# A hybrid attention layer on one core: the first gate block's weight split tied behind the attention output, the norm weights spread by TensorE, and the opening order of VectorE changed

## The chip, the cores and the metric

The kernel runs on one core of one Trainium2 chip. The metric is the device time of one execution in microseconds (us); it is given as the median of several executions. A profile of one further execution has a span (first to last instruction) that is a little shorter than that execution's own time. Engines are named as in the profile: PE is TensorE, PEld its weight loads, DVE VectorE, ACT ScalarE, POOL GpSimd, SP SyncE, which issues most transfers (DMA).

## What is computed

One transformer layer on 512 tokens of width 1024, all in float32:

```python
h = rmsnorm(x, norm_mix_w)                    # (512, 1024)
z = h @ w_in                                  # 2328 columns: u, v, q, three k/v pairs, gates
a = gmlp_group(u, v, ...)                     # gated mixing inside chunks of 128 tokens, 8 heads
b = nsa_group(q, k_c, v_c, k_s, v_s, k_w, v_w, g_raw, ...)   # compressed, selected, window attention
mix = concat([rmsnorm(a, out_norm_a_w), rmsnorm(b, out_norm_b_w)])
x = x + mix @ w_o
h = rmsnorm(x, norm_ffn_w)
x = x + (silu(h @ w_gate) * (h @ w_up)) @ w_down            # inner width 2816
out = rmsnorm(x, final_norm_w)
```

## The kernel before

**Precision.** A float32 product is made of three matmuls of a reduced format. Each operand is split into a high part (an ACT copy, `copy_a`, line 79) and a low part (a subtraction, `sub`, line 76, mostly on DVE), and `mm3` (lines 114 to 116) adds high by high, high by low and low by high. Every weight block is therefore loaded (`load_raw`, line 87, into one of three raw buffers), split by two instructions (`split`), and only then read by PE. A raw buffer is free for the next transfer once its low part is made.

**Opening.** Tokens come in four tiles `t` of 128. SP issues the transfers of `x` and of the v columns of `w_in` (`wv`) alternately, and after the first `x` tile that of `wbn`, the norm weights `norm_mix_w`, read once for each of the 128 partitions. `START` writes out the order in which ACT and DVE do four steps per tile: `S` (sums of squares on ACT, then the reciprocal root on POOL, line 167), `T` (DVE scales the tile's two halves by root and weight, line 174, and PE transposes them, line 178), `W` (split of the v weights of that number) and `K` (the transposed tile is split into `hTh` and `hTl`). PE then multiplies: `z_v` is the v projection, 96 matmuls of 512 columns. Ahead of it PE runs 24 transposes of the identity (`warm`, line 199) which nothing reads.

**Attention and output projection.** Scores, softmax (`P`), transposes of the probabilities (`ptp`, line 621), their split (`PT`, high on ACT, low on DVE) and the product with the values (`o`, line 641) go unit by unit; units are numbered (PT46 is the last). After the last unit the raw output `oraw3` is put together (DVE line 650) and split into `mixbh` and `mixbl`, and `pto` (line 660) transposes it for the norm. The output projection `po` (`project`) fills PE's gaps: its first half uses `mixa` and needs no attention, its second half uses `mixb` and the weights `wo1..`, whose low parts POOL makes. Then `ffn_norm(t)` forms the second norm of each tile: squares on ACT (`xf`), root on POOL, DVE scaling by `fwb` (line 174), PE transposes `pt_f`, split into `h2h` and `h2l`.

**Feed-forward.** `gate_up(f)` loads and splits the gate and up blocks of 128 columns, f = 0 to 21; `gate_up(0, 0)` and `gate_up(0, 1)` do block 0 in two token halves while the norm of the last tile is still being made. Its two splits are `wg0` and `wu0`. The splits of block 1 are tied behind `last_norm` by an order-only dependency (`after`): the scheduler must place the later instruction behind the earlier one, and no semaphore is added.

Engines run their instructions in the order that the scheduler wrote, so an instruction that waits holds up all that stand behind it on its engine. Names in rows carry no buffer numbers: `wg_s` is wg0's split, `wo_s` a split of an output weight.

Of the kernel before, what the change touches and what calls it, by code (L numbers as in the profile page):

```python
# [8 lines left out]
F32 = mybir.dt.float32  # L9
F32R = mybir.dt.float32r  # L10
AF = mybir.ActivationFunctionType
OP = mybir.AluOpType
# [6 lines left out]
P = 128  # L19
S = 512  # L20
NT = S // P
DM = 1024
KD = DM // P
# [7 lines left out]
C_U, C_V, C_Q, C_KC, C_KS, C_KW, C_G = 0, 512, 1024, 1536, 1792, 2048, 2304  # L31
NG = 24
FFN_GROUPS = (4, 6, 6, 6)
START = (("S", 0), ("T", 0), ("W", 0), ("K", 0), ("S", 1), ("W", 1), ("T", 1), ("S", 2), ("K", 1), ("T", 2),
         ("W", 2), ("S", 3), ("K", 2), ("T", 3), ("W", 3), ("K", 3))
BANKS = (3, 2, 2, 1)
NBIG, NP, NRAW, NSPL, T4, T2 = 11, 3, 3, 4, 3, 4
# [4 lines left out]
def hybrid_gmlp_nsa_kernel(  # L42
# [8 lines left out]
    nc = tc.nc  # L51
    x, out = x[0], out[0]
    w_in, w_o, w_gate, w_up, w_down = w_in[0], w_o[0], w_gate[0], w_up[0], w_down[0]

    cp = ctx.enter_context(tc.tile_pool(name="consts", bufs=1))
# [19 lines left out]
    def sub(o, a, hi, eng=None):  # L75
        return (eng or nc.vector).tensor_tensor(out=o, in0=a, in1=hi.bitcast(F32), op=OP.subtract)  # L76

    def copy_a(o, a):
        return nc.scalar.activation(o, a, AF.Copy)  # L79
# [25 lines left out]
    def load_cols(w, r0, nk, c0, n, name, eng=None, spare=False, behind=None, halves=False):  # L105
        src = w[r0:r0 + nk * P, c0:c0 + n].rearrange("(k p) f -> p k f", p=P)
        return split(load_raw(src, [nk, n], name), [nk, n], name, eng, spare, behind, halves)

    def after(later, earlier):
        tc.add_manual_dep(later.ins, earlier.ins.name,  # L110
                          mybir.DependencyInfo(mybir.DependencyClass.NoSync, mybir.DependencyReason.DATA), reason="order")
# [6 lines left out]
    def bcast_row(vec, n, name, tag=None):  # L118
        t = cp.tile([P, DM if tag else n], F32, name=name, tag=tag or name)[:, :n]
        nc.sync.dma_start(t, bass.AP(tensor=vec.tensor, offset=vec.offset, ap=[[0, P], [1, n]]))  # L120
        return t
# [4 lines left out]
    def xt(t):  # L126
        return x_sb[t // 2][:, t % 2]

    def v_raw(t):
        return load_raw(w_in[t * 256:(t + 1) * 256, C_V:C_V + 512].rearrange("(k p) f -> p k f", p=P),  # L130
                        [2, 512], f"wv{t}")

    wv_raw = []
    for t in range(NT):
        nc.sync.dma_start(xt(t), x[t * P:(t + 1) * P])
        if t == 0:
            wbn = bcast_row(norm_mix_w, DM, "wbn", tag="wb")
        if t < NRAW:
            wv_raw.append(v_raw(t))

    ident = cp.tile([P, P], F32, name="ident")
    make_identity(nc, ident)
    mhalf = cp.tile([P, 1], F32, name="mhalf")
    nc.vector.memset(mhalf, -0.5)

# [24 lines left out]
    def norm_turn(x_t, r, wb, xs, name):  # L170
        pts = []
        for hf in range(2):
            c = slice(hf * 512, hf * 512 + 512)
            nc.vector.scalar_tensor_tensor(out=xs[:, c], in0=x_t[:, c], scalar=r, in1=wb[:, c],
                                           op0=OP.mult, op1=OP.mult)
            pt = bank("T", [P, 4, P], f"pt_{name}_{hf}")
            for k in range(4):
                nc.tensor.transpose(pt[:, k], xs[:, (hf * 4 + k) * P:(hf * 4 + k + 1) * P], ident)
            pts.append(pt)
        return pts  # L180

    def norm_keep(pts, dst_h, dst_l, t):
        for hf, pt in enumerate(pts):
            d = (slice(None), slice(None), slice(t * P, (t + 1) * P))
            copy_a(dst_h[hf][d], pt)
            done = sub(dst_l[hf][d], pt, dst_h[hf][d])
        return done
# [6 lines left out]
    def bank(tag, shape, name):  # L194
        return ps.tile(shape, F32, tag=tag, name=name, bufs=NB[tag])

    warm = bank("O", [P, 4, P], "warm")
    for k in range(24):
        nc.tensor.transpose(warm[:, k % 4], ident, ident)
    hTh = [b8([P, 4, S], F32R, f"hTh{a}") for a in range(2)]  # L200
    hTl = [b8([P, 4, S], F32R, f"hTl{a}") for a in range(2)]
    v_units = []
    with tc.manual_schedule(engines={mybir.EngineType.Activation, mybir.EngineType.DVE}):
        xs, rs, pts = {}, {}, {}

        def start(t):
            xs[t] = t4([P, DM], F32, f"xs{t}")
            rs[t] = rstd_halves(xt(t), xs[t], f"x{t}")

        def turned(t):  # L210
            pts[t] = norm_turn(xt(t), rs[t], wbn, xs[t], f"x{t}")

        def weight(t):
            if t >= NRAW:
                wv_raw.append(v_raw(t))
            v_units.append(split(wv_raw[t], [2, 512], f"wv{t}"))

        for op, t in START:
            if op == "K":
                norm_keep(pts[t], hTh, hTl, t)  # L220
            else:
                {"S": start, "T": turned, "W": weight}[op](t)

# [18 lines left out]
    for t, z in enumerate(zs):  # L242
# [4 lines left out]
        r = rstd_of(ssq, DA, f"v{t}")  # L247
# [51 lines left out]
    NX = NKV * NCMP  # L299
# [16 lines left out]


    sel = cp.tile([2 * NX, NX], F32, name="sel")
    nc.vector.tensor_tensor(out=sel, in0=ident[:2 * NX, 0:NX], in1=ident[:2 * NX, NX:2 * NX], op=OP.add)
    pair = cp.tile([P, 2, 32], F32, name="pair")  # L320
    idv = ident.rearrange("p (a e n) -> p a e n", a=2, e=2)
    nc.vector.tensor_tensor(out=pair, in0=idv[:, :, 0], in1=idv[:, :, 1], op=OP.add)
    pair = pair.rearrange("p a n -> p (a n)")
    KC = cp.tile([P, NKV, 2, P], F32R, name="KC")
    VC = cp.tile([P, NKV, P], F32R, name="VC")
# [94 lines left out]
    ws = t4([P, NH, P], F32, "ws")  # L420
# [12 lines left out]
    for h2 in range(NH // 2):  # L433
        sv = bank("S", [P, 2, NT, HD], f"sv{h2}")
        for hh in range(2):
            h = h2 * 2 + hh
            c = slice(h * HD, (h + 1) * HD)
            mm3(sv[:, hh], wsT[:, 0, h], wsT[:, 1, h], vnh[:, :, c], vnl[:, :, c], True, True)
            nc.vector.scalar_tensor_tensor(out=ua[:, :, c], in0=sv[:, hh], scalar=bsT[:, h:h + 1],
                                           in1=ua[:, :, c], op0=OP.add, op1=OP.mult)  # L440
# [8 lines left out]
    for k in range(4):  # L449
        pt = bank("T", [P, NT, P], f"pta{k}")  # L450
        for t in range(NT):
# [4 lines left out]
                                       in1=mixah[:, k].bitcast(F32), op0=OP.mult, op1=OP.subtract)  # L456
# [153 lines left out]
    PTs, PTC, outs, oraws, rstd_b = {}, {}, {}, {}, [None] * NT  # L610
# [20 lines left out]
    def apply(u):  # L631
        gi, j, br = UNITS[u]
        i, kv, b0 = GROUPS[gi]
        first, last = j == 0 and b0 + br == 0, j is None
        if first:
            outs[i, kv] = bank("O", [P, 4, P], f"o_{i}{kv}")
        o = outs[i, kv]
        of = o.rearrange("p h c -> p (h c)")
        if not last:
            for a in range(2):  # L640
                nc.tensor.matmul(of, lhsT=Vt[:, b0 + br, j, kv], rhs=PTs[u][:, a],  # L641
                                 start=(first and a == 0), stop=False)
            return
        nc.tensor.matmul(of, lhsT=VC[:, kv], rhs=PTC[i], start=False, stop=True)
        if kv == 0:
            oraws[i] = tp.tile([P, 4, P], F32, tag="oraw", name=f"oraw{i}", bufs=2)
        ol = t2([HD, 4, P], F32, f"ol_{i}{kv}")
        copy_a(ol, o[HD:P])
        for par in range(2):
            nc.vector.tensor_tensor(out=oraws[i][par * HD:(par + 1) * HD, 2 * kv:2 * kv + 2],  # L650
                                    in0=o[0:HD, par::2], in1=ol[:, par::2], op=OP.add)
        if kv == 1:
            d = (slice(None), slice(None), slice(i * P, (i + 1) * P))
            copy_a(mixbh[d], oraws[i])
            sub(mixbl[d], oraws[i], mixbh[d])

    def out_norm(i):
        pt = bank("T", [P, 4, P], f"pto{i}")
# [6 lines left out]
    def ffn_norm(t):  # L665
        xs = t4([P, DM], F32, f"xf{t}")
        r = rstd_halves(x2[t], xs, f"f{t}")
        pts = norm_turn(x2[t], r, fwb, xs, f"f{t}")
        return norm_keep(pts, h2h, h2l, t)


# [33 lines left out]
    gu = {}  # L705

    def gate_up(f, part=None):
        if not part:
            ws = [load_cols(w, 0, KD, f * P, P, f"w{'gu'[a]}{f}", spare=f == 0, behind=last_norm if f == 1 else None,
                            halves=f > 0)  # L710
                  for a, w in ((0, w_gate), (1, w_up))]
            gu[f] = ws, [bank("G" if part is None else "S", [P, S], f"gu{f}{a}") for a in range(2)]
        cut = slice(0, S) if part is None else slice(part * 256, part * 256 + 256)
        for (hi, lo), z in zip(*gu[f]):
            for k in range(KD):
                mm3(z[:, cut], hi[:, k], lo[:, k], h2h[k // 4][:, k % 4, cut], h2l[k // 4][:, k % 4, cut],
                    k == 0, k == KD - 1)
# [28 lines left out]
    last_norm = ffn_norm(NT - 1)  # L746
# [143 lines left out]
```

## Time and profile before

| | before |
|---|---|
| median of 3 executions | 624.6 us (622.62, 624.6, 624.99) |
| the profiled execution's own time | 623.25 us |
| its span | 621.5 us |
| mean granted TensorE clock | 0.991 |
| PE busy | 597.8 us, 96% |
| DVE busy | 401.7 us, 65% |
| ACT busy | 297.4 us, 48% |
| POOL busy | 68.5 us, 11% |

The page gives each engine's busy time as a share of the span. 1.75 us lie between the span and the execution's own time. Times in rows are microseconds from the start of the span; mean durations of one instruction are in ns.

### The profile page before, as it was taken

The numbers are of one execution on the slowest core, as the hardware profiler recorded it, in microseconds if no ns is written. First come the engines' busy times: TensorE is split into PE (matmuls) and PEld (weight loads), VectorE is DVE, ScalarE is ACT, GpSimd is POOL, SyncE is SP. The second block draws the span as 40 slices with busy tenths as digits, with TensorE's granted clock in tenths as the row PEclk, the third lists the DMA queues.
The fourth block names the chain that finished last, engine by engine and source line by source line (L and its number), as shares of the span: only waits on it lengthen the run. The fifth ranks groups of instructions, "written<-read, shape, count | busy, mean of one in ns | idle before, by whom it ended". The sixth has DMA issues, their size and how long they took to land.

```text
span 621.5 us, 7683 instructions
## 1 busy us (share of the span) xinstructions
PE 597.8 (96%) x2823; PEld 489.5 (79%) x2823; DVE 401.7 (65%) x728; ACT 297.4 (48%) x547; POOL 68.5 (11%) x113
## 2 busy tenths in 40 slices
PE   6999899998999988999999999999999999999994
PEld 5778778787788766898888888888888888888883
DVE  4752779648988956646694437694446695346696
ACT  5753367648877865344252323353233353233354
POOL 3100100015442571100000000000000000000001
PEclk9999999999999997999999999999999999999998
DMA  8551635533000021069118232028232018320003
GB/s 314 154 142 51 182 107 150 188 125 115 1 2 1 1 63 40 1 174 320 48 44 261 82 94 62 1 89 266 86 100 69 1 70 270 101 67 1 0 2 135
DMA packets 73638, 61.85 MB, mean 100 GB/s; under 512 B 3697, under 2 KB 64129, under 8 KB 73601
## 3 DMA queue, kind: packets, MB, share of 16 engines
q1 hardware_dynamic: 73024, 60.32, 31.1%
q10 hardware_dynamic: 576, 1.05, 0.4%
q8 instruction: 22, 0.36, 0.2%
q14 instruction: 16, 0.12, 0.1%
HBM read 59.27 MB, written 2.10 MB: 99 GB/s over the span
## 4 chain that ended last, share of the span: by engine, by line
PE 84%; DVE 4%; DMA 3%; ACT 3%; POOL 3%; issue 2%; SPq 0%; POOLq 0%; ACTq 0%; DVEq 0%
PE gu L115 13%; PE gu L116 13%; PE gu L114 13%; PE o L641 3%; PE pA L114 3%; PE pA L116 3%; PE pA L115 3%; PE s L547 3%; PE ptp L621 3%; PE po L115 2%; PE po L116 2%; PE po L114 2%; PE pC L116 1%; PE pC L115 1%; PE pC L114 1%
## 5 line engine op out<-in xcount | busy, mean ns | idle before, releaser
L114 PE MATMUL gu<-h2h,wg_h 128*128 128x512 f32 x168 | 65.4, 389 | 0.0
L115 PE MATMUL gu<-h2l,wg_h 128*128 128x512 f32 x168 | 65.4, 389 | 0.0
L115 PE MATMUL gu<-h2l,wu_h 128*128 128x512 f32 x168 | 65.4, 389 | 0.0
L116 PE MATMUL gu<-h2h,wg_l 128*128 128x512 f32 x168 | 65.4, 389 | 0.0
L114 PE MATMUL gu<-h2h,wu_h 128*128 128x512 f32 x168 | 65.4, 389 | 0.0
L116 PE MATMUL gu<-h2h,wu_l 128*128 128x512 f32 x168 | 65.4, 389 | 0.0
L79 ACT ACTIVATE wu_h<-wu_r 128x1024 fp32r<-128x1024 f32 x21 | 22.3, 1061 | 64.7 <-PE gu L115 48.8
L690 DVE TENSOR_TENSOR sg<-gu,sg 128x512 f32<-128x512 f32 x22 | 15.2, 691 | 57.3 <-PE gu L116 56.7
L76 DVE TENSOR_TENSOR wg_l<-wg_r,wg_h 128x1024 fp32r<-128x1024 f32 x21 | 25.7, 1223 | 41.0 <-ACT wg_h L79 40.5
L79 ACT ACTIVATE wg_h<-wg_r 128x1024 fp32r<-128x1024 f32 x21 | 22.3, 1060 | 48.0 <-PE gu L115 40.9
L167 POOL TENSOR_TENSOR rstd_y<-s_y,mhalf 128x1 f32<-128x1 f32 x4 | 3.0, 754 | 346.1 <-DVE s_y L164 341.4
L552 ACT ACTIVATE P<-P,nm 128x128 f32<-128x128 f32 (+3 forms) x64 | 35.5, 559 | 5.2 <-DVE nm L550 4.7
L82 POOL TENSOR_SCALAR P<-P,sm 128x128 f32<-128x128 f32 (+3 forms) x64 | 34.0, 552 | 32.2 <-DVE sm L559 15.0
L116 PEld LDWEIGHTS gu<-h2h,wg_l 128*128 128x128 f32 x168 | 31.5, 188 | 6.6
L116 PEld LDWEIGHTS gu<-h2h,wu_l 128*128 128x128 f32 x168 | 31.5, 188 | 6.6
L115 PEld LDWEIGHTS gu<-h2l,wu_h 128*128 128x128 f32 x168 | 31.6, 188 | 6.5
L114 PEld LDWEIGHTS gu<-h2h,wg_h 128*128 128x128 f32 x168 | 31.6, 188 | 6.5
L114 PEld LDWEIGHTS gu<-h2h,wu_h 128*128 128x128 f32 x168 | 31.5, 188 | 6.5
L115 PEld LDWEIGHTS gu<-h2l,wg_h 128*128 128x128 f32 x168 | 31.5, 188 | 6.5
L641 PE MATMUL o<-PT,Vt 128*128 128x512 f32 x80 | 32.0, 451 | 4.8 <-ACT PT L79 4.6
L550 DVE CUSTOM_DVE_ANT_0 P<-s,maskw 128x128 f32<-128x128 f32 (+3 forms) x64 | 29.5, 481 | 4.1 <-PE s L547 3.6
L76 DVE TENSOR_TENSOR wu_l<-wu_r,wu_h 128x1024 fp32r<-128x1024 f32 x21 | 25.6, 1219 | 4.9 <-ACT wu_h L79 4.9
(505 smaller groups left out, 1504.7 us busy)
## 6 DMA issues: line engine op xcount, KB each, us to landing
wg_r<-in_w_gate_dram SPq DMA_DIRECT2D x22, 512.0 KB, 3.9
wu_r<-in_w_up_dram SPq DMA_DIRECT2D x22, 512.0 KB, 3.8
wd_r<-in_w_down_dram SPq DMA_DIRECT2D x11, 1024.0 KB, 5.0
wo_r<-in_w_o_dram SPq DMA_DIRECT2D x8, 512.0 KB, 4.3
x_sb<-in_x_dram SPq DMA_DIRECT2D x4, 512.0 KB, 9.0
wv_r<-in_w_in_dram SPq DMA_DIRECT2D x4, 512.0 KB, 7.7
wu_r<-in_w_in_dram SPq DMA_DIRECT2D x4, 512.0 KB, 3.7
w1k_r<-in_cmp_k_w_dram SPq DMA_DIRECT2D x4, 512.0 KB, 3.8
```

What stands on the lines that cost most here:

```text
L76: return (eng or nc.vector).tensor_tensor(out=o, in0=a, in1=hi.bitcast(F32), op=OP.subtract)
L79: return nc.scalar.activation(o, a, AF.Copy)
L82: nc.gpsimd.tensor_scalar(out=o, in0=a, scalar1=s, scalar2=1.0, op0=OP.mult, op1=OP.mult)
L114: nc.tensor.matmul(ps, lhsT=sh, rhs=mh, start=first, stop=False, skip_group_check=more)
L115: nc.tensor.matmul(ps, lhsT=sh, rhs=ml, start=False, stop=False, skip_group_check=more)
L116: nc.tensor.matmul(ps, lhsT=sl, rhs=mh, start=False, stop=last, skip_group_check=more)
L547: nc.tensor.matmul(sb, lhsT=q, rhs=KAB[kv][:, a, b0:b0 + nbr, :n], start=(a == 0), stop=(a == 1))
L550: nc.vector.tensor_tensor_reduce(out=pr, in0=sb[:, br], in1=maskw[:, S - n:], scale=-0.125, scalar=BIG, op0=OP.add, op1=OP.min, accum_out= ...
L552: e = nc.scalar.activation(pr, pr, AF.Exp, bias=nm[b], scale=-1.0, accum_out=sm[b])
L621: nc.tensor.transpose(pt[:, hh], src, ident)
L641: nc.tensor.matmul(of, lhsT=Vt[:, b0 + br, j, kv], rhs=PTs[u][:, a], start=(first and a == 0), stop=False)
L690: nc.vector.tensor_tensor(out=own, in0=pg[1], in1=own, op=OP.mult)
```

## The change

Three things are changed.

1. The split of the gate and up weights of block 0 gets an order-only dependency on the low part of the last attention output, `mixbl` of tile 3, which is the last entry of the new list `mixed`. Before it had none.
2. The transfer that wrote `norm_mix_w` into all 128 partitions is gone. One row of 4 KB is loaded into one partition by ACT's queue (`wrow`), and two plain float32 matmuls with a row of ones spread it over the partitions into two PSUM banks (`wbn[0]`, `wbn[1]`), from where DVE reads it. The 24 warm transposes become 6 ahead of the spread and 3 behind it.
3. On DVE, `T` of tile 1 now stands ahead of `W` of tile 1, and the two small sums `sel` and `pair` are tied behind the last `hTl` of the opening.

```diff
-START = (("S", 0), ("T", 0), ("W", 0), ("K", 0), ("S", 1), ("W", 1), ("T", 1), ("S", 2), ("K", 1), ("T", 2),
+START = (("S", 0), ("T", 0), ("W", 0), ("K", 0), ("S", 1), ("T", 1), ("W", 1), ("S", 2), ("K", 1), ("T", 2),
...
+    wrow = cp.tile([P, DM], F32, name="wrow", tag="wb")
+    nc.scalar.dma_start(wrow[0:1], bass.AP(tensor=norm_mix_w.tensor, offset=norm_mix_w.offset, ap=[[0, 1], [1, DM]]))
     for t in range(NT):
         nc.sync.dma_start(xt(t), x[t * P:(t + 1) * P])
-        if t == 0:
-            wbn = bcast_row(norm_mix_w, DM, "wbn", tag="wb")
...
-            nc.vector.scalar_tensor_tensor(out=xs[:, c], in0=x_t[:, c], scalar=r, in1=wb[:, c],
+            nc.vector.scalar_tensor_tensor(out=xs[:, c], in0=x_t[:, c], scalar=r, in1=wb[hf],
...
-    for k in range(24):
-        nc.tensor.transpose(warm[:, k % 4], ident, ident)
+    for k in range(6):
+        warmed = nc.tensor.transpose(warm[:, k % 4], ident, ident)
+    wbn = []
+    for hf in range(2):
+        wbn.append(bank("SM"[hf], [P, 512], f"wbn{hf}"))
+        spread = nc.tensor.matmul(wbn[hf], lhsT=ones, rhs=wrow[0:1, hf * 512:hf * 512 + 512], start=True, stop=True)
+        after(spread, warmed)
+    for k in range(3):
+        after(nc.tensor.transpose(warm[:, k % 4], ident, ident), spread)
...
-            sub(mixbl[d], oraws[i], mixbh[d])
+            mixed.append(sub(mixbl[d], oraws[i], mixbh[d]))
...
-            ws = [load_cols(w, 0, KD, f * P, P, f"w{'gu'[a]}{f}", spare=f == 0, behind=last_norm if f == 1 else None,
-                            halves=f > 0)
+            behind = mixed[-1] if f == 0 else last_norm if f == 1 else None
+            ws = [load_cols(w, 0, KD, f * P, P, f"w{'gu'[a]}{f}", spare=f == 0, behind=behind, halves=f > 0)
```

The first place where instructions move is ACT at the end of the attention, from the copy of probability unit 43 on. Before:

```order
L79 ACTIVATE PT43_2184<-ptp43_2179 128x512
L79 ACTIVATE wg0_s_2564<-wg0_r_2562 128x1024
L79 ACTIVATE PT44_2194<-ptp44_2189 128x512
L79 ACTIVATE PT45_2204<-ptp45_2199 128x512
L79 ACTIVATE wo111_s_2375<-wo111_r_2371 128x1024
L79 ACTIVATE wu0_s_2569<-wu0_r_2567 128x1024
L79 ACTIVATE PT46_2214<-ptp46_2209 128x512
L79 ACTIVATE ol_31_2220<-o_31_2146 64x512
```

And now:

```order
L79 ACTIVATE PT43_2175<-ptp43_2170 128x512
L79 ACTIVATE PT44_2185<-ptp44_2180 128x512
L79 ACTIVATE PT45_2195<-ptp45_2190 128x512
L79 ACTIVATE wo111_s_2366<-wo111_r_2362 128x1024
L79 ACTIVATE PT46_2205<-ptp46_2200 128x512
L79 ACTIVATE ol_31_2211<-o_31_2137 64x512
L79 ACTIVATE mixbh_1166<-oraw3_2095 128x4x128
L157 ACTIVATE junko3_2222,ssq_o3_2223<-pto3_2217 128x512
L164 ACTIVATE xf0_2425,s2_f0_2426<-x2_0_1168 128x512
L79 ACTIVATE wg0_s_2555<-wg0_r_2553 128x1024
L79 ACTIVATE wu0_s_2560<-wu0_r_2558 128x1024
L164 ACTIVATE xf0_2425,s2_f0_2426<-x2_0_1168 128x512
```

The copies of wg0 and wu0 moved from between the last probability copies to between the two halves of the squares of the first feed-forward norm tile.

The second place is DVE a little later, from the last attention output to the scaling of the first feed-forward norm tile (`xf0`). In the kernel before, the two splits stood ahead of this piece, the first behind PT43 and the second behind PT45. Now:

```order
L661 TENSOR_TENSOR oraw3_2095<-o_31_2137,ol_31_2211 64x256 x2
L524 SCALAR_TENSOR_TENSOR x2_0_1168<-po100_2369,rstd_o0_1454,x2_0_1168 128x512
L76 TENSOR_TENSOR mixbl_1167<-oraw3_2095,mixbh_1166 128x4x128
L150 TENSOR_SCALAR ms_o3_2225<-ssq_o3_2223 128x1
L166 TENSOR_SCALAR s2_f0_2426<-s2_f0_2426 128x1
L524 SCALAR_TENSOR_TENSOR x2_0_1168<-po101_2383,rstd_o0_1454,x2_0_1168 128x512
L76 TENSOR_TENSOR wg0_s_2555<-wg0_r_2553,wg0_s_2555 128x1024
L76 TENSOR_TENSOR wu0_s_2560<-wu0_r_2558,wu0_s_2560 128x1024
L524 SCALAR_TENSOR_TENSOR x2_0_1168<-po110_2397,rstd_o1_1657,x2_0_1168 128x512
L168 TENSOR_TENSOR s2_f0_2426<-s2_f0_2426 128x1
L176 SCALAR_TENSOR_TENSOR xf0_2425<-x2_0_1168,rstd_f0_2430,fwb_1174 128x512 x2
```

The low parts of wg0 and wu0 now stand between the first tile's squares and its scaling.

The third place is the start of DVE's program. Before:

```order
L76 TENSOR_TENSOR wv0_s_145<-wv0_r_75,wv0_s_145 128x1024
L319 TENSOR_TENSOR sel_546<-ident_84 124x62
L322 TENSOR_TENSOR pair_548<-ident_84 128x64
L76 TENSOR_TENSOR hTl0_121<-pt_x0_0_134,hTh0_119 128x4x128
L76 TENSOR_TENSOR hTl1_122<-pt_x0_1_140,hTh1_120 128x4x128
L164 TENSOR_SCALAR s2_x1_153<-s2_x1_153 128x1
L166 TENSOR_TENSOR s2_x1_153<-s2_x1_153 128x1
L76 TENSOR_TENSOR wv1_s_160<-wv1_r_78,wv1_s_160 128x1024
L174 SCALAR_TENSOR_TENSOR xs1_152<-x_sb0_70,rstd_x1_157,wbn_73 128x512 x2
```

And now:

```order
L76 TENSOR_TENSOR wv0_s_136<-wv0_r_75,wv0_s_136 128x1024
L76 TENSOR_TENSOR hTl0_112<-pt_x0_0_125,hTh0_110 128x4x128
L76 TENSOR_TENSOR hTl1_113<-pt_x0_1_131,hTh1_111 128x4x128
L166 TENSOR_SCALAR s2_x1_144<-s2_x1_144 128x1
L168 TENSOR_TENSOR s2_x1_144<-s2_x1_144 128x1
L176 SCALAR_TENSOR_TENSOR xs1_143<-x_sb0_70,rstd_x1_148,wbn0_103 128x512
L176 SCALAR_TENSOR_TENSOR xs1_143<-x_sb0_70,rstd_x1_148,wbn1_105 128x512
L76 TENSOR_TENSOR wv1_s_163<-wv1_r_78,wv1_s_163 128x1024
```

The scaling of tile 1 (`xs1`) changed places with the split of wv1, and `sel` and `pair` left this stretch.

## Rows read from the trace of the kernel before

**Rows 1.** The page's first part: busy time, share of the span, instructions.
```profile
PE 597.8 (96%) x2823; PEld 489.5 (79%) x2823; DVE 401.7 (65%) x728; ACT 297.4 (48%) x547; POOL 68.5 (11%) x113
```

**Rows 2.** Waits of PE, whole span: total us, times, longest.
```profile
PE o L641 <- ACT PT L79: 4.6, 1, 4.6
```

**Rows 3.** Busy us of PE, PEld, DVE, ACT, POOL, then PEclk, DMA, GB/s.
```profile
238.00:240.00 2.00, 2.00 (x8) 1.52 (x8) 2.00 (x2) 0.16 (x1) 1.67 (x1) 0.50 0.01 4
242.00:244.00 2.00, 2.00 (x10) 1.65 (x9) 0.22 (x1) 0.46 (x1) 0.00 (x0) 1.00 0.00 0
400.00:500.00 100.00, 100.00 (x441) 82.41 (x440) 62.48 (x88) 36.65 (x50) 0.00 (x0) 1.00 0.30 95
```

**Rows 4.** Timeline, end of attention: start, us, instruction, [idle before <-releaser].
```profile
230.75 0.47 PE L116 MATMUL po<-wo_s,mixal 128*128 128x512 f32 x1
234.24 1.06 ACT L79 ACTIVATE wg_s<-wg_r 128x1024 fp32r<-128x1024 f32 x1 [5.32 <-DMA wg_r<-in_w_gate_dram]
235.20 1.06 ACT L79 ACTIVATE PT<-ptp 128x512 fp32r<-128x512 f32 x2
235.32 1.23 DVE L76 TENSOR_TENSOR wg_s<-wg_r,wg_s 128x1024 fp32r<-128x1024 f32 x1 [5.68 <-ACT wg_s L79]
235.83 0.79 PE L641 MATMUL o<-PT,Vt 128*128 128x512 f32 x1 [4.60 <-ACT PT L79]
236.42 0.63 PE L114 MATMUL po<-wo_s,mixbh 128*128 128x512 f32 x1
236.85 0.63 PE L115 MATMUL po<-wo_s,mixbh 128*128 128x512 f32 x1
237.29 2.38 POOL L76 TENSOR_TENSOR wo_s<-wo_r,wo_s 128x1024 fp32r<-128x1024 f32 x1 [4.72 <-ACT wo_s L79]
238.26 2.49 DVE L76 TENSOR_TENSOR wu_s<-wu_r,wu_s 128x1024 fp32r<-128x1024 f32 x1
...
245.39 0.39 PE L660 MATMUL pto<-ident,oraw 128*128 128x128 f32 x2
245.98 0.69 DVE L76 TENSOR_TENSOR mixbl<-oraw,mixbh 128x512 fp32r<-128x512 f32 x1 [0.45 <-ACT mixbh L79]
248.53 0.55 POOL L167 TENSOR_TENSOR rstd_f<-s_f,mhalf 128x1 f32<-128x1 f32 x1 [1.06 <-DVE s_f L166]
252.01 1.03 PE L178 MATMUL pt_f<-ident,xf 128*128 128x128 f32 x8
```

**Rows 5.** Timeline of the opening.
```profile
4.18 0.63 ACT L162 ACTIVATE xs<-x_sb 128x512 f32<-128x512 f32 x1 [2.12 <-DMA x_sb<-in_x_dram]
5.80 0.56 POOL L167 TENSOR_TENSOR rstd_x<-s_x,mhalf 128x1 f32<-128x1 f32 x1 [4.01 <-DVE s_x L166]
6.69 1.41 DVE L174 SCALAR_TENSOR_TENSOR xs<-x_sb,rstd_x,wbn 128x512 f32<-128x512 f32 x2 [0.98 <-DMA wbn<-in_norm_mix_w_dram]
8.23 1.06 ACT L79 ACTIVATE wv_s<-wv_r 128x1024 fp32r<-128x1024 f32 x1 [2.71 <-DMA wv_r<-in_w_in_dram]
9.20 1.07 ACT L79 ACTIVATE hTh<-pt_x 128x512 fp32r<-128x512 f32 x2
10.47 0.22 DVE L319 TENSOR_TENSOR sel<-ident 124x62 f32<-124x62 f32 x1
13.61 1.40 DVE L174 SCALAR_TENSOR_TENSOR xs<-x_sb,rstd_x,wbn 128x512 f32<-128x512 f32 x2
13.75 0.50 PE L115 MATMUL z_v<-wv_s,hTh 128*128 128x512 f32 x1 [0.76 <-DVE wv_s L76]
```

**Rows 6.** Weight loads of PE in the opening, timeline.
```profile
1.84 4.57 PEld L199 LDWEIGHTS warm<-ident 128*128 128x128 f32 x24 [1.84 <-POOL ident masks.py:199]
7.50 0.42 PEld L178 LDWEIGHTS pt_x<-ident,xs 128*128 128x128 f32 x4 [1.09 <-DVE xs L174]
```

**Rows 7.** Groups by form: name, shape, count, busy us, mean ns, idle before.
```profile
L580 PE MATMUL ptc<-pair,st_sb 128*128 128x64 f32 x32 | 4.2, 265 | 0.0
L513 DVE SCALAR_TENSOR_TENSOR x<-po,rstd_o,x 128x512 f32<-128x512 f32 x8 | 6.0, 748 | 2.8 <-PE po L116 2.8
```

More of the change, by code (lines that the diff above doesn't have):

```diff
@@ L142, in hybrid_gmlp_nsa_kernel @@
     make_identity(nc, ident)
+    ones = cp.tile([1, P], F32, name="ones")
+    nc.vector.memset(ones, 1.0)
     mhalf = cp.tile([P, 1], F32, name="mhalf")
@@ L219, in hybrid_gmlp_nsa_kernel @@
             if op == "K":
-                norm_keep(pts[t], hTh, hTl, t)
+                kept = norm_keep(pts[t], hTh, hTl, t)
             else:
@@ L318, in hybrid_gmlp_nsa_kernel @@
     sel = cp.tile([2 * NX, NX], F32, name="sel")
-    nc.vector.tensor_tensor(out=sel, in0=ident[:2 * NX, 0:NX], in1=ident[:2 * NX, NX:2 * NX], op=OP.add)
+    done = nc.vector.tensor_tensor(out=sel, in0=ident[:2 * NX, 0:NX], in1=ident[:2 * NX, NX:2 * NX], op=OP.add)
+    after(done, kept)
     pair = cp.tile([P, 2, 32], F32, name="pair")
     idv = ident.rearrange("p (a e n) -> p a e n", a=2, e=2)
-    nc.vector.tensor_tensor(out=pair, in0=idv[:, :, 0], in1=idv[:, :, 1], op=OP.add)
+    done = nc.vector.tensor_tensor(out=pair, in0=idv[:, :, 0], in1=idv[:, :, 1], op=OP.add)
+    after(done, kept)
     pair = pair.rearrange("p a n -> p (a n)")
@@ L654, in apply @@
             copy_a(mixbh[d], oraws[i])
-            sub(mixbl[d], oraws[i], mixbh[d])
+            mixed.append(sub(mixbl[d], oraws[i], mixbh[d]))
+    mixed = []
     def out_norm(i):
@@ L667, in ffn_norm @@
         r = rstd_halves(x2[t], xs, f"f{t}")
-        pts = norm_turn(x2[t], r, fwb, xs, f"f{t}")
+        pts = norm_turn(x2[t], r, (fwb[:, 0:512], fwb[:, 512:]), xs, f"f{t}")
         return norm_keep(pts, h2h, h2l, t)
```

## The prediction

> **What bounds the kernel now.** I read the page's busy shares first: PE is busy 96% of the span, every other engine far less [rows 1]. So the time is PE's work plus the moments in which PE has none or runs slowly, and a change pays only there. The waits of PE come next. The longest single one is a product `o` that waits 4.6 us for the ACT copy of a probability tile [rows 2]; the other waits are small, most of them in the opening.
>
> The timeline around that wait shows who is to blame. PE ends its last free output-projection matmul at about 231.0 (it starts at 230.75, and in long dense stretches 441 matmuls take 100 us, 0.227 each) [rows 3, 4]. The transposes for PT44 and PT45 are done by then, but on ACT the copy of wg0 stands ahead of both, and waits 5.32 us for its transfer, which lands at 234.2. PT44 and PT45 run from 235.20, and PE starts again at 235.83. So the 4.6 us come from an instruction that nobody needs for another 30 us.
>
> The stretch behind it costs more. [...] What the stall costs in all follows from a count: from 231.0 until `pto` at 245.39, PE does, by the order of its instructions, 27 matmuls and 6 transposes. At 0.227 and 0.105 (four transposes' loads take 0.42 [rows 6]) that is 6.1 + 0.6 = 6.75 us. It took 14.4. The excess is 7.65: 4.6 of standing still and about 3.05 of slow clock.
>
> Last I read the opening. DVE's first scaling waits for `wbn` until 6.69, although its root is ready at 5.80 + 0.56 = 6.36; the first v weights follow wbn on the queue and land at 8.23, where ACT has waited 2.71 for them [rows 5]. At 13.75 PE waits its last 0.76 for the low part of wv1, and from there it is nearly closed.
>
> **The change, part by part.**
>
> *The tie behind mixbl.* ACT now goes from PT43 straight to PT44 and PT45. Their transposes end at about 230.5 and 231.0, so the high parts (two take 1.06 [rows 4]) come at 231.15 and 231.75 and DVE's low parts, 0.69 each, at 231.85 and 232.5. PE meanwhile has `o` with the high parts and three projection matmuls; by the order it meets each low part within 0.1 us. The copy of wo111 now runs at 231.8 to 232.8 instead of 236.15, so POOL, whose 2.38 us for its low part began at 237.29 [rows 4], ends near 235.2; PE needs it at about 238.0. That wait, which could have taken the old one's place, stays hidden with 2.8 us to spare. I leave 0.2 us for small waits: 7.65 - 0.2 = 7.45 gained. With no idle stretch the clock has no reason to drop.
>
> *The splits in their new place.* Two ACT copies (1.06 each) and two DVE subtractions (1.23 each [rows 4]) now stand inside the first feed-forward norm. Let p be the time at which PE reaches the second pair of `pto`. Until `pt_f` of tile 0 PE then has 2 transposes and 33 matmuls: p + 7.7. On the other side the add for x2's second half waits for nine more matmuls and ends at p + 3.1 (0.75 [rows 7]). ACT copies wg0 from p + 2.1 and wu0 until p + 4.25, and DVE makes their low parts until p + 5.7. Behind them stand the next add (0.75, to 6.45), the sum of squares, POOL's root (0.55 [rows 4]) with its semaphores (to 7.3) and the first scaling (0.75, to 8.05). PE waits 0.35 there, and 0.35 more since the second half comes 0.75 later and four transposes cover 0.42. I take 0.75 lost. In the kernel before, `pt_f` began at 252.01, 6.6 after `pto`, without a wait. The other tiles' scalings come one by one behind 5.5 us of matmuls each and keep their cover. The bounds: 0 if ACT and DVE run a little ahead of this, and 3.25 if both subtractions take 2.49 each, as that of wu0 did while POOL was at work beside it [rows 4]. In the new place POOL has only roots of 0.55, so 1.23 is nearer.
>
> Together 7.45 - 0.75 = **6.7 us** at this place (bounds 4.2 and 7.65).
>
> *The row instead of the broadcast.* The first x tile lands at 4.18, wbn only at about 6.6 [rows 5]. Without it everything queued behind moves up 2.4 us; wv0 lands near 5.9, and ACT need not wait at 8.23. The row itself is not in the trace. Its landing lies between 0 and the 3.4 us that the 512 KB of x needed from its issue at 0.79: 4.2 at the latest. The spread is two plain float32 matmuls. The nearest rows: a plain float32 matmul leaves two records (32 for 16 calls [rows 7]), and a 128-column transpose takes 4.57/24 = 0.19 at the start and 0.105 later [rows 6]. A 512-column record is then four times that, and the spread 4 x 0.42 = 1.7 to 4 x 0.76 = 3.0; below, 0.9 if a record takes the 0.227 of a dense matmul. So the halves are in PSUM between about 4 and 7.2; DVE wants them at 6.4 and 7.1. Reading the weights from PSUM costs nothing that rows show: 748 ns with a PSUM operand [rows 7] against 1.41 us for two from SBUF [rows 5].
>
> [...]
>
> *DVE's order.* With wv0 there early, hTh of tile 0 is bound by its transposes and starts near 7.7 (9.20 before). `sel` and `pair` (0.22 each) leave DVE. Scaling of tile 1 starts at about 11.4 instead of 13.61 (its root is ready at 11.3), while the low part of wv1, behind it, ends at 14.0 instead of 13.7. When PE closes up, at 14.0, it has done 9 of the 96 z_v matmuls and 16 of 32 transposes, against 7 and 8 at 13.75: 2 x 0.227 + 8 x 0.105 - 0.25 = 1.05 gained. Following DVE to its last hTl instead gives 1.3. With the spread at its latest, PE's 3 warm transposes delay `pt_x` of tile 0 by 0.8, and 0.5 to 0.7 is left. I take **1.0 us** (bounds -0.8, with spread and clock both at their slow end, and 2.4, the whole of wbn's transfer). From 14 on PE is closed, and the transfers of the u weights hang on buffers that PE's progress frees, so the gain reaches the attention unchanged.
>
> *Sum.* 1.0 + 6.7 = 7.7. The profiled execution took 623.25; 615.5 for such a one. The median of the runs is 1.35 higher, 624.6, so **616.9 us**. A difference under about 0.5% (3 us) could not be told from no change here.
>
> **Rivals.**
>
> *A: the wait moves to pt_f.* The splits are slow, PE stands 3.25 us at `pt_f`, and 7.7 - 2.5 = 5.2 are left: 619.4; 622.2 if the clock then falls as it did behind the 4.6 (another 2.8). For it: DVE's 2.49 [rows 4]. Against it: POOL is done by then.
>
> *B: the opening loses.* 15 fewer warm transposes and a hole while PE waits for the row leave PE at the lower clock when z_v begins. After the old stall some 13 matmuls ran slowly, 0.2 us each too long: 2.6. Then the opening is 1.6 worse instead of 1.0 better: 619.5. For it: the early transposes take 0.19, later ones 0.105, so PE did start slowly [rows 6]. Against it: z_v's first matmuls wait for ACT and DVE anyway.
>
> *C: slower.* The same mechanism without an end in sight: z_v's beginning stays so thin that the clock stays low through it. At 0.2 us each it needs 38 slow matmuls to eat the 7.7 and 54 to be slower by 0.5%; all 96 give 616.9 + 19.4 = 636. Against it: after the old stall PE resumed at 235.83 and the clock was back at 1.00 in 242 to 244 [rows 3, 4].
>
> [...]
>
> *D: the opening gains all.* The whole 2.4 of wbn comes through: 615.5.
>
> **How the numbers follow.** The forecast has 0.70, A 0.10, B 0.12, C 0.03, D 0.05. The time is the forecast's, 616.9. The range goes down to D less the spread of the runs (0.8 us below their middle mostly): 614.5. Upward it takes in A and B with as much again: 620.3. Outside lie C, A with the low clock and outliers. Faster by over 0.5% means under 621.5: the forecast, D, most of A and B: 0.93. Within it 0.04, slower 0.03.
>
> **What would show it.** Right: no PE wait for PT of more than 0.5 us; a granted clock of 1.00 from 225 to 250; wg0's copy behind the first half of xf0's squares; `pto` to `pt_f` 7.5 to 9 us; z_v's last matmul 0.5 to 1.5 us earlier. Wrong: a wait at `pt_f` over 2 us, z_v matmuls 0.43 apart beyond the first dozen, DVE's first scaling later than 7, or a new PE wait for POOL's wo111.

## The result, and the profile after

The changed kernel takes 616.91 us in the median of 4 runs (616.63 to 618.19), the kernel before 624.29 (622.62 to 624.99) beside it: a ratio of 0.989, 95% interval 0.9865 to 0.9915, so 5.3 to 8.4 us less. The forecast was 616.9. The profiled execution took 617.18 with a span of 615.4, against 623.25 and 621.5: 6.1 less. The total came out as forecast; several of its terms did not, and the experiments are about those.

The first fence is from the page after (busy time), PE's waits, and PE's busy time and granted clock in the stretch of the old stall (columns as in [rows 3]).

```profile
PE 598.2 (97%) x2812; PEld 487.3 (79%) x2812; DVE 400.7 (65%) x729; ACT 297.7 (48%) x547; POOL 68.2 (11%) x113
...
PE ptp L632 <- POOL P L82: 2.8, 5, 0.8
...
PE cps_v L384 <- ACT hid_v L366: 0.4, 1, 0.4
PE z_u L115 <- DVE wu_s L76: 0.4, 1, 0.4
...
PE pt_x L180 <- DVE xs L176: 0.3, 1, 0.3
PE z_v L114 <- ACT wv_s L79: 0.2, 1, 0.2
...
230.00:240.00 10.00, 9.98 (x50) 7.47 (x49) 5.17 (x10) 5.16 (x11) 5.96 (x4) 1.00 0.36 105
240.00:250.00 10.00, 9.96 (x48) 8.00 (x47) 8.12 (x14) 5.04 (x10) 1.31 (x3) 1.00 0.00 0
```

The wait of `o` for PT [rows 2] is gone, no PE wait is over 0.8 us longest but the two fixed ones on POOL's `ident` (1.8) and `ws` (1.6), and the granted clock that was 0.50 [rows 3], with matmuls 0.43 apart instead of 0.227 [rows 3, 4], is 1.00 throughout. The timeline after, in the place of [rows 4]:

```profile
231.16 1.09 ACT L79 ACTIVATE PT<-ptp 128x512 fp32r<-128x512 f32 x2 [1.64 <-PE ptp L632]
231.32 0.47 PE L116 MATMUL po<-wo_s,mixal 128*128 128x512 f32 x1
231.81 0.50 PE L652 MATMUL o<-PT,Vt 128*128 128x512 f32 x1
...
239.28 0.62 ACT L164 ACTIVATE xf<-x 128x512 f32<-128x512 f32 x1
239.90 1.05 ACT L79 ACTIVATE wg_s<-wg_r 128x1024 fp32r<-128x1024 f32 x1
240.85 1.05 ACT L79 ACTIVATE wu_s<-wu_r 128x1024 fp32r<-128x1024 f32 x1
241.27 1.22 DVE L76 TENSOR_TENSOR wg_s<-wg_r,wg_s 128x1024 fp32r<-128x1024 f32 x1
242.40 1.22 DVE L76 TENSOR_TENSOR wu_s<-wu_r,wu_s 128x1024 fp32r<-128x1024 f32 x1
245.01 1.41 DVE L176 SCALAR_TENSOR_TENSOR xf<-x,rstd_f,fwb 128x512 f32<-128x512 f32 x2 [0.67 <-POOL rstd_f L169]
245.91 1.29 PE L180 MATMUL pt_f<-ident,xf 128*128 128x128 f32 x8
246.96 0.47 PE L114 MATMUL po<-wo_s,mixbh 128*128 128x512 f32 x1
...
259.63 0.36 PE L114 MATMUL gu<-h2h,wg_s 128*128 128x256 f32 x1
```

`o` follows the free projection matmul after 0.5 instead of 5.1 us. The copies of wg0 and wu0 stand behind the first half of xf0's squares, as forecast, and both low parts take 1.22, not 2.49. From the start of that free matmul to `pt_f` of tile 0 it is 14.59 us (231.32 to 245.91), before it was 21.26 (230.75 to 252.01): 6.67 less. By the order of instructions the same 56 matmuls and 8 transposes lie in both; at 0.227 and 0.105 they are 13.54 us. The excess over that was 7.72 and is 1.05.

The forecast of 6.7 took in what is lost behind the start of `pt_f` too, so the fair end is the first gate matmul `gu`. It starts at 259.63; before it was

```profile
265.48 0.36 PE L114 MATMUL gu<-h2h,wg_s 128*128 128x256 f32 x1
```

That is 34.73 us from the free matmul before and 28.31 now: **6.42 less, where 6.7 was forecast**. The span shows 6.1: the free matmul itself comes 0.57 later in this execution than in the one before, and 0.25 is won behind `gu`.

The opening after, in the place of [rows 5, 6]:

```profile
3.31 3.77 PE L205 MATMUL wbn<-wrow,ones 1*128 1x512 f32 x4
6.58 1.40 DVE L176 SCALAR_TENSOR_TENSOR xs<-x_sb,rstd_x,wbn 128x512 f32<-128x512 f32 x2 [0.68 <-POOL rstd_x L169]
7.71 1.91 PE L180 MATMUL pt_x<-ident,xs 128*128 128x128 f32 x8
8.81 0.60 ACT L79 ACTIVATE hTh<-pt_x 128x512 fp32r<-128x512 f32 x1 [2.10 <-PE pt_x L180]
9.46 0.79 PE L114 MATMUL z_v<-wv_s,hTh 128*128 128x512 f32 x1
10.05 0.63 PE L115 MATMUL z_v<-wv_s,hTh 128*128 128x512 f32 x1
10.47 0.63 PE L116 MATMUL z_v<-wv_s,hTl 128*128 128x512 f32 x1
12.35 1.40 DVE L176 SCALAR_TENSOR_TENSOR xs<-x_sb,rstd_x,wbn 128x512 f32<-128x512 f32 x2 [0.68 <-POOL rstd_x L169]
12.48 0.49 PE L114 MATMUL z_v<-wv_s,hTh 128*128 128x512 f32 x1 [0.23 <-ACT wv_s L79]
```

The row is there by 3.31, so it does land early; but the spread takes 3.77, and PE works at half its pace long behind it: `pt_x` takes 1.91 instead of 1.32 and the first z_v matmuls stand 0.43 apart. (The windows of this opening say a granted clock of 1.00 throughout, also where the matmuls stand 0.43 apart, so here the pace is read from their distance.) ACT waits 2.10 for `pt_x`, and the scaling of tile 1 comes at 12.35 where 11.4 was forecast. The first matmul of z_u, which follows z_v without a gap, starts at 36.83 instead of 37.24: 0.4 gained, not 1.0.

And this 0.4 does not reach the end of the attention: on ACT the copy of w_k stands ahead of `hid_v`, and its transfer came late.

```profile
111.48 1.06 ACT L79 ACTIVATE w_k_s<-w_k_r 128x1024 fp32r<-128x1024 f32 x1 [0.86 <-DMA w_k_r<-in_w_in_dram]
112.45 0.25 ACT L366 ACTIVATE hid_v<-hps_v 128x124 f32<-128x124 f32 x1
112.75 0.63 PE L384 MATMUL cps_v<-w_v,hid_v 128*31 128x64 f32 x8 [0.44 <-ACT hid_v L366]
```

`cps_v` starts at 112.75, before at 112.76. This goes mostly with the new opening: PE waits 0.2 to 0.6 at this place in all six traces in which the new opening brought the first z_u matmul before 37 (after, and e2, e5, e8, e11 and e12 of the experiments below), and of the eight others only in e4, 0.4. Why the transfer is late there stays open; an early z_u alone does not do it, since e7, which has the earliest, has no such wait.

### The profile page after: what moved, and what is told of

Its sections match the earlier page's. It is cut to its first block, busy times and chain, and to the rows that moved or that the text cites. A ratio compares the mean times of both kernels' runs of the same rounds, so it can differ in the third digit from the quotient of the medians.

```text
span 615.4 us, 7662 instructions
## 1 busy us (share of the span) xinstructions
PE 598.2 (97%) x2812; PEld 487.3 (79%) x2812; DVE 400.7 (65%) x729; ACT 297.7 (48%) x547; POOL 68.2 (11%) x113
## 3 DMA queue, kind: packets, MB, share of 16 engines
q10 hardware_dynamic: 578, 1.05, 0.5%
## 4 chain that ended last, share of the span: by engine, by line
PE 87%; DVE 5%; DMA 2%; POOL 2%; ACT 2%; issue 1%; POOLq 0%; SPq 0%; DVEq 0%; ACTq 0%
PE gu L115 13%; PE gu L116 13%; PE gu L114 13%; PE o L652 3%; PE pA L114 3%; PE ptp L632 3%; PE pA L115 3%; PE pA L116 3%; PE s L558 3%; PE po L115 2%; PE po L116 2%; PE po L114 2%; PE pC L114 2%; PE pC L115 2%; PE pC L116 2%
## 5 line engine op out<-in xcount | busy, mean ns | idle before, releaser
L76 DVE TENSOR_TENSOR PT<-ptp,PT 128x512 fp32r<-128x512 f32 x40 | 26.6, 684 | 5.7 <-ACT PT L79 5.5
```

## The experiments

**One part alone.** First the tie without the opening, and the opening without the tie.

```
# e1: before, and
+            mixed.append(sub(mixbl[d], oraws[i], mixbh[d]))
+            behind = mixed[-1] if f == 0 else last_norm if f == 1 else None
# e2: the changed kernel, with these two undone
```

> The kernel before with the tie behind mixbl alone. Theory (the prediction's terms): -6.7 us, about 617.6 at a median of 624.3, no PE wait for PT, granted clock 1.00 from 225 to 250, pto to pt_f 7.5 to 8. Rival (the opening earned the gain, or the two parts need each other): under 4 us gained here.

> The kernel before with the row, the spread and DVE's order, without the tie. The prediction's term: -1.0 us, 623.3. Theory after the two traces: the gain is 0.5 at the first z_u matmul (36.8 against 37.2) and is taken back at cps_v, where ACT waits for the transfer of w_k_r; 0 in the end, 624.3 +- 0.5. Rival B (the slow PE costs more than the transfer gives): 1.6 worse, 626.

e1: 617.43 against 623.13, ratio 0.9901 (0.9883 to 0.992). e2: 622.94 against the same, ratio 0.9996 (0.9986 to 1.0006). So the tie earns 5 to 7.3 us, and the opening between a loss of 0.4 and a gain of 0.9. In e1's trace, too, it is 14.59 us from the free matmul to `pt_f`. e2's first z_u matmul is at 36.85, and PE waits 0.2 at `cps_v`, so part of that gain is taken back there, as was expected of e2. e1's, which has the opening of before, is at 38.86, 1.6 later than in the execution of before that was profiled (below, matmuls of z_v and windows with columns as in [rows 3]):

```profile
12.15 0.63 PE L114 MATMUL z_v<-wv_s,hTh 128*128 128x512 f32 x1
12.57 0.63 PE L115 MATMUL z_v<-wv_s,hTh 128*128 128x512 f32 x1
...
8.00:10.00 2.00, 0.88 (x7) 0.51 (x5) 0.68 (x2) 1.69 (x3) 1.10 (x4) 1.00 1.04 413
12.00:14.00 2.00, 2.00 (x6) 1.22 (x6) 1.78 (x5) 1.73 (x5) 0.56 (x1) 0.50 1.04 391
14.00:17.00 3.00, 3.00 (x12) 2.42 (x12) 1.32 (x5) 0.60 (x1) 0.55 (x1) 0.50 0.93 279
```

With the same code and the same 24 transposes, PE went through z_v's beginning at half its pace until 17 this time: after a stretch in which it was busy 0.88 of 2 us (0.98 in before) the granted clock fell to 0.50. In e3 it reads 0.50 from 12 to 14, in before 1.00 throughout. So the opening of before is not one number; the three other traces with it (before, e3, e4) have the first z_u matmul at 37.17 to 37.59. With the new opening (after, e2, and e5 below) it is at 36.83, 36.85 and 36.86.

**What the stall cost.** e3 keeps the stall and gives PE something to do in it; e4 leaves the copies untied and takes their transfers away.

```
# e3: before, and in the loop over units, between turn(45) and apply(44);
# not shown: the first o is tied behind the last pad, PT46's transposes behind o
+    pad, prev = bank("S", [P, 4, P], "pad"), turn(45)
+    for k in range(44):
+        pad_mm = nc.tensor.transpose(pad[:, k % 4], ident, ident)
+        after(pad_mm, prev)
+        prev = pad_mm
# e4: before, and in load_cols
+    if spare:
+        return split(fwb.rearrange("p (k f) -> p k f", k=nk), [nk, n], name, eng, spare, behind, halves)
```

> The kernel before with 44 transposes of the identity, into a bank that nobody reads, between the transposes of PT45 and the product o that waits for PT44; PT46's transposes go behind o. The stall stays (ACT still waits for wg0's transfer until 234.2), PE only has something to do in it. Theory (the 3 us behind the stall come from PE having stood still): granted clock stays 1.00 and matmuls 0.227 apart behind 236, about 3 us gained, 621.3. [...]

> The kernel before with wg0 and wu0 split from a tile that landed long ago (the norm's weights), so that their transfers are gone and the first gate block's result is another; no tie, so ACT still has the copies ahead of the PTs. Theory (the wait for the transfer made the stall, not the 1.06 us of each copy): no PE wait for PT over 0.8 us, and no new work inside the first feed-forward norm, 7.5 gained, 616.8. Rival (ACT simply has too much ahead of PT44): a wait of 1 to 2 us stays, with a slow clock behind it, 619 to 621.

e3: 623.04, ratio 1.0 (0.9987 to 1.0012): no gain, yet the clock did not fall. Its timeline of PE, and the window in which the clock was 0.50 before:

```profile
230.95 4.97 PE L744 MATMUL pad<-ident 128*128 128x128 f32 x44
235.76 0.50 PE L644 MATMUL o<-PT,Vt 128*128 128x512 f32 x1
237.14 1.09 PE L644 MATMUL o<-PT,Vt 128*128 128x512 f32 x3 [0.88 <-DVE PT L76]
...
238.00:240.00 2.00, 2.00 (x12) 1.41 (x12) 1.66 (x3) 1.29 (x2) 0.00 (x0) 1.00 0.00 0
```

The granted clock stays 1.00, and behind 238 the matmuls stand 0.227 apart. So the slow clock did come from PE standing still, and 4.8 us of nothing but transposes kept it away; only transposes had run, too, when the loads went from 0.19 to 0.105 us [rows 6]. The count of the same work tells where the gain went: from 230.95 to `pt_f` at 251.29 it is 20.34 us (21.26 before), 6.80 over the 13.54. Of this 4.81 are the transposes put in, 1.15 lie at the new wait (in this kernel's order `o` meets PT44's low part at once, which on DVE stands behind wg0's), and 0.84 remain. So 0.84 of excess is what this stretch costs at full clock, in steps of about 0.1 where PE changes between `po`, `o` and transposes. Before had 7.72 = 4.85 at the stall + 2.87, and by this count the slow clock's share of the 2.87 is about 2.0. Counted by instructions it is 2.6: nine matmuls take 0.20 too long each, a tenth 0.15, and six transposes 0.105 each. Either is less than the 3.05 of the prediction.

e4: 617.83, ratio 0.992 (0.9903 to 0.9937), 4 to 6 us gained. This run changes one thing more: the scheduler puts the copies earlier, behind PT41 and PT42 instead of PT43 and PT45. They still stand ahead of probability copies of the same kind, 1.06 us each, and PE waits for none of those on ACT. But something of the rival is there, on DVE instead of ACT:

```profile
227.87 9.05 POOL L76 TENSOR_TENSOR wo_s<-wo_r,wo_s 128x1024 fp32r<-128x1024 f32 x3
229.51 2.82 DVE L76 TENSOR_TENSOR wu_s<-fwb,wu_s 128x1024 fp32r<-128x1024 f32 x1
232.26 1.27 DVE L76 TENSOR_TENSOR PT<-ptp,PT 128x512 fp32r<-128x512 f32 x2
232.99 0.73 PE L643 MATMUL o<-PT,Vt 128*128 128x512 f32 x2 [1.25 <-DVE PT L76]
```

Beside POOL's subtraction of the same kind wu0's low part takes 2.82, in the changed kernel without POOL 1.22. The low part of a probability tile waits behind it, and PE 1.25. This is rival A's mechanism, found where POOL does work. The transfer made most of the stall; in this order the place next to POOL still costs 1.3 us.

**What the opening is made of.** Beside the changed kernel once more (e5), e6 takes DVE's order back, e9 (later) puts that order alone into the kernel before, e7 leaves the norm's weights out, and e8 uses ACT's idle 2.1 us.

```
# e5: the changed kernel
# e6: START with ("W", 1), ("T", 1) again; e9: before with ("T", 1), ("W", 1) and sel, pair behind kept
# e7: no wrow, no spread; 24 transposes; ones = cp.tile([P, DM], F32, ...) set to 1
+    wbn = [ones[:, 0:512], ones[:, 512:]]
# e8: START = ... ("W", 0), ("S", 1), ("K", 0), ("T", 1), ("W", 1), ...
```

> The changed kernel itself once more, as the measure for the others here: 616.9 +- 1. Its opening: first z_v matmul about 9.5, z_v 0.43 apart until about 12, first z_u matmul near 36.8. If one of these differs by more than 0.3, the opening varies from execution to execution and single profiles do not price it.

> The changed kernel with DVE's old opening order (low part of wv1 ahead of the scaling of tile 1). Theory (the order is worth something, since the scaling of tile 1 goes from 12.35 to about 13.6): first z_u matmul 0.3 to 1.0 later than in the changed kernel, total 617.2 to 617.9. Rival (PE has z_v matmuls of tile 0 to do meanwhile and the order is worth nothing): within 0.2.

> The changed kernel without row and spread: the norm's weights are left out (a tile of ones in SBUF takes their place), 24 transposes stand at the start as before the change, DVE's new order stays. The bound of what the opening could give. Theory (the slow pace of PE through pt_x and z_v took half of the predicted 1.0): pt_x 0.105 each, z_v 0.227 apart from the start, first z_u matmul 0.5 to 1.2 earlier than in the changed kernel, total about 616. Rival (pace does not matter, ACT and DVE set z_v's beginning): within 0.2 at z_u.

> The changed kernel with the squares of x tile 1 ahead of the copies of hTh 0 on ACT, which stands idle for 2.1 us there. x1 should have landed by about 7.1 (wv0 is copied at 5.66, and 512 KB take 1.4 at 370 GB/s). Theory: scaling of tile 1 at about 11 instead of 12.35, first z_u matmul 0.5 to 1.0 earlier, total 616.0 to 616.4. Rival (x1 lands later than 8, the squares delay hTh): first z_v matmul later than 9.5 and no gain or 0.5 lost.

> The kernel before with DVE's new opening order alone (scaling of tile 1 ahead of the low part of wv1; sel and pair behind the last hTl), with the broadcast and the 24 transposes as they were. Theory (the order earned the opening's 0.4 and row plus spread earned nothing, since the changed kernel with the old order has its first z_u matmul at 37.4 against 37.2 before): first z_u matmul at 36.5 to 36.9 where PE's pace in the opening is 0.227, total 0.3 to 0.7 under before, 622.4. Rival (the order helps only with the weights there early): 37.2, no gain.

e5 repeats the changed kernel's opening to within 0.06. The starts of the first z_v and z_u matmul in the traces, with the median of the runs (e5 to e8 on one chip with a median of before of 622.92, e9 against 623.07):

```
                              first z_v   first z_u   median us   ratio (95%)
before                           9.83       37.24
e5 changed kernel again          9.49       36.86       616.32    0.9885 (0.9864 to 0.9907)
e6 with DVE's old order          9.46       37.44       616.86    0.9898 (0.9877 to 0.992)
e9 before, new order alone       9.75       37.27       622.72    0.9988 (0.9974 to 1.0002)
e7 weights left out              8.58       35.85       614.88    0.9867 (0.9843 to 0.989)
e8 squares of tile 1 early       9.87       36.21       615.62    0.9877 (0.9856 to 0.9898)
```

Differences of 0.5 us in the medians are inside the intervals; the starts carry these readings, and each is from one execution. With weights and spread gone (e7) `pt_x` takes 1.32 and z_v is quick from the beginning:

```profile
7.17 1.32 PE L178 MATMUL pt_x<-ident,xs 128*128 128x128 f32 x8
8.58 0.50 PE L114 MATMUL z_v<-wv_s,hTh 128*128 128x512 f32 x1
...
10.00 0.39 PE L114 MATMUL z_v<-wv_s,hTh 128*128 128x512 f32 x1
10.23 0.40 PE L115 MATMUL z_v<-wv_s,hTh 128*128 128x512 f32 x1
```

So without the spread the opening would be worth 1.4 at z_u, and the spread with PE's slow pace behind it takes 1.0 of them. Of the rest, neither half stands alone: the row without the order (e6) is at 37.44, the order without the row (e9) at 37.27, both no better than before; together they are at 36.83 to 36.86 in three traces. As single executions of one opening differ by up to 0.7 (e8 and e11 below), this is likely and not shown. The reason for e6 stands in its rows: DVE makes wv1's low part from 12.46 and scales tile 1 at 13.61 as before, and PE waits 0.65 for that low part. In e9 the rival is right: with the broadcast still ahead of the v weights the scaling comes at 12.68, but PE runs out of z_v matmuls and waits 0.66 for it.

In e8 x tile 1 lands at 8.0, not at the 7.1 that I had worked out, so the first z_v matmul is 0.4 later; the scaling of tile 1 comes at 11.05 all the same and z_u 0.65 earlier. The median fell by 0.7, inside the interval. In e11, with the same opening, z_u was back at 36.88 with the first z_v matmul as late: there PE kept its slow pace longer (the eight transposes of tile 1 take 1.31, in e8 1.03). The gain is not settled.

**The spread's slow pace.** e10 spreads over all 128 rows; e12 over 97, with the row loaded as early as in the changed kernel. e11 and e12 also tie the splits further back.

```
# e10: nc.vector.memset(wrow, 0.0) ahead of the load; ones = cp.tile([P, P], ...); rhs=wrow[:, ...]; 12 transposes
# e12: row into wrow[96:97]; nc.vector.memset(wrow[0:96], 0.0); ones = cp.tile([97, P], ...); rhs=wrow[0:97, ...]
# e11 (with e8's START) and e12
+            behind = norm0[0] if f == 0 else last_norm if f == 1 else None
+            norm0.append(ffn_norm(t - 1))
```

> The changed kernel with the spread over all 128 rows: the tile of the row is set to 0 first, ones is 128x128, and 12 transposes stand ahead of it, since the row now comes about 1 us later. Same result, same two calls. Theory (a matmul with one row of weights did not bring PE to its quick pace, one with 128 rows does, as the transposes did): z_v 0.227 apart from the start, first z_v matmul at 8.9 to 9.4, first z_u matmul 0.4 to 0.9 earlier than in the changed kernel (36.84), total 615.5 to 616. Rival (rows make no difference): z_v 0.43 apart until 12 or later, first z_u matmul at 37 or later since the spread ends later.

> The changed kernel with the squares of x tile 1 ahead of hTh 0 (as in e8) and the tie of wg0 and wu0 behind the last h2l of tile 0 instead of mixbl. Theory (the splits delay the second half of pt_f of tile 0 by 0.25, and have 12 us of room behind it): pt_f of tile 0 to the first gu matmul 13.5 instead of 13.72, no new PE wait, 615.4 against the 615.6 of e8. Rival (the splits now delay tile 1's norm or the first gu matmul): over 13.8.

> The changed kernel with the row loaded into partition 96 at the same time as before, partitions 0 to 95 of its tile set to 0 and the spread over 97 rows, the six transposes ahead of it as they were; and wg0 and wu0 tied behind the last h2l of tile 0 instead of mixbl. Theory (one row does not bring PE to its quick pace, 97 do): z_v 0.227 apart from the start or nearly, first z_v matmul 8.7 to 9.1 (9.46), first z_u matmul 36.0 to 36.3 (36.84); pt_f of tile 0 to the first gu matmul 13.50; 615.3 to 615.7 in all. Rival (rows make no difference, the 12 transposes ahead of the spread in e10 did it): z_v 0.43 apart until 12, first z_u matmul at 36.8, 616.1.

e10: 618.19, ratio 0.9911 (0.989 to 0.9933). Here the row is issued at 2.02, behind the first loads of x and the v weights, and PE waits 2.25 for it until 6.91; issued at 0.79 it was there by 3.31. That costs the 2 us (the first z_u matmul is at 39.03). The pace behind the spread is quick, but z_v begins only at 11.82 here, so this decides little. e12 has the row on time and differs from the changed kernel's opening only in the rows and the two memsets:

```profile
3.35 3.75 PE L206 MATMUL wbn<-wrow,ones 97*128 97x512 f32 x4
7.53 1.92 PE L181 MATMUL pt_x<-ident,xs 128*128 128x128 f32 x8
9.29 0.58 PE L114 MATMUL z_v<-wv_s,hTh 128*128 128x512 f32 x1
9.71 0.39 PE L115 MATMUL z_v<-wv_s,hTh 128*128 128x512 f32 x1
...
10.58 0.40 PE L115 MATMUL z_v<-wv_s,hTh 128*128 128x512 f32 x1
10.81 0.40 PE L116 MATMUL z_v<-wv_s,hTl 128*128 128x512 f32 x1
12.31 0.50 PE L114 MATMUL z_v<-wv_s,hTh 128*128 128x512 f32 x1 [1.10 <-ACT wv_s L79]
...
145.00:150.00 5.00, 3.12 (x16) 1.95 (x15) 3.66 (x22) 3.87 (x19) 4.26 (x10) 0.94 0.03 11
150.00:155.00 5.00, 5.00 (x19) 4.22 (x20) 2.55 (x12) 3.74 (x12) 2.21 (x5) 0.72 0.00 0
```

z_v is quick from about 9.7 on, in the changed kernel from about 12: with 97 rows instead of one in the spread PE reached its quick pace over 2 us earlier. This is one execution, against six with one row (after, e2, e5, e6, e8, e11), all of which still had 0.43 between z_v matmuls at 11. It brings less than expected, since `pt_x` was still slow, hTh and with it wv1's copy on ACT come hardly earlier (11.21 against 11.38), and PE, quicker now, waits 1.10 for that copy; z_u is at 36.61. The last two lines show why e12's profiled execution took 618.3 for all that: PE waits for POOL's scaled probabilities and is busy 3.12 of 5 us in 145 to 150, and then the granted clock falls to 0.72. e11's profiled execution has the same (3.74 of 5, then 0.66). The other traces have these waits without a drop, the changed kernel's with 3.17 of 5.

The medians are 617.08 for e11, ratio 0.9891 (0.9868 to 0.9915), and 615.97 for e12, ratio 0.9879 (0.9856 to 0.9902). The later tie does what it should: from `pt_f` of tile 0 to the first gu matmul it is 13.50 in both (13.72 in the changed kernel, 13.47 before). No version is shown to beat the changed kernel; e8 and e12 have lower medians than e5 by 0.7 and 0.35, within the intervals.

## Why the prediction was right

**The place.** Right: the gain that is clear of noise comes from the tie (e1), 6.42 up to the first gate matmul against 6.7 forecast. The mechanism is confirmed from both sides: without the transfer most of the stall is gone though copies still stand ahead of the probability tiles (e4), and with PE at work in it the clock stays up (e3).

**The total.** That it agrees to 0.01 us is luck. The forecast took 7.7 off a median of 624.6 from three runs. In the experiments, with more runs, before had medians of 622.9 to 623.1, and the changed kernel beside them gained 6.6 (e5): the forecast gain was about 1 too large, most of it in the opening, and its base lay high by about as much.

**Its terms** were off and made up for each other. The slow clock was put at 3.05 and is 2.0 to 2.6: I had taken everything over 0.227 and 0.105 for slow clock. But from 231.0 to 235.83 it is 4.83 of standing still and not 4.6, and up to 0.85 is what such an order costs at full clock too (e3; 1.05 with the small waits in the changed kernel, for which the prediction had 0.2). The new wait at `pt_f` was put at 0.75: the first half of `pt_f` does not wait at all, and the second half and what follows cost 0.25 (e11, e12). The chain that I added up there came out shorter: the first scaling ends at about 245.7, 7.65 behind `pto` instead of 8.05, since the low parts ended 0.15 earlier than I had it and each link behind them gave up to 0.1 more; and PE reaches `pt_f` 7.85 behind `pto` instead of 7.7.

**The opening** was put at 1.0 with bounds from -0.8 to 2.4. The measurement says -0.4 to 0.9, the traces 0.4 at z_u. The failed step is the cost of `pt_x`: I let hTh of tile 0 start at 7.7, with transposes of 0.105. PE had not come to its quick pace when `pt_x` began, hTh started at 8.81, and all behind it moved by that much. Rival B named this, with a price of 2.6; it is 1.0 (e7). The spread itself took 3.77, over its upper bound of 3.0; it still ended inside the bounds, at about 7.1, since the row landed early. Reading the weights from PSUM cost nothing: two scalings take 1.40, before 1.41.

**"The gain reaches the attention unchanged"** failed: at `cps_v` PE waits 0.2 to 0.6 for ACT in every trace with this opening's early z_u, which takes back much or all of its 0.4. In all, single executions differ by up to 1.1 us between the first z_u matmul and `cps_v` (75.3 to 76.4), and by up to 1.0 from there to the first `ptp` (34.0 to 35.0), whatever the opening did.

Of the signs named in advance, all at the old stall came true, `pto` to `pt_f` with 7.85 too; z_v's end moved by 0.4, just short of the 0.5 named.

## What to carry to other kernels

A weight split that nobody needs yet, placed in front of copies that TensorE waits for, can cost the transfer's wait plus a stretch of slow clock behind it (here 4.85 us and 2.0 to 2.6); tie it behind the last thing that must not wait, and not beside GpSimd's work of the same kind (here a low part took 2.82 us beside it in e4, 1.22 without it in the changed kernel). When you cost a slow stretch by counting instructions, take the count's pace from a stretch with the same mixture, not from a dense one (here 0.84 us of difference over 56 matmuls and 8 transposes, e3). Replacing a transfer by work on an engine that is still at its slow pace can give back much of what the transfer cost (here 1.0 of 1.4 us); try it with the weights left out first (e7) to see what there is to win, and each half alone, since two edits may pay only together.

## What was not expected of the hardware

The spread takes 3.77 us with one row and 3.75 with 97, but behind the one z_v stood 0.43 apart until about 12, behind the other (in one execution) 0.23 to 0.34 from 9.7 on. The same 24 transposes with a pause behind them were followed by the quick pace in one execution and by a granted clock of 0.50 from 12 to 17 in another (z_u at 37.24 and 38.86); over the 23 runs of before beside e1 the times went from 621.44, at a mean granted clock of 0.995, to 625.13 at 0.986, while the 11 runs of e2, where PE has no such pause, lay between 622.08 and 623.41 at 0.990 to 0.993. And a row of 4 KB that was issued 1.2 us later, behind the first loads of x, landed at least 3.6 us later.
